# A conformer block on one core: the opening rebuilt on a transposed copy of x, three gate tiles moved to the front, and the fifth score row cut at another column

## The chip, the cores and the metric

The kernel runs on one core of a Trainium2 chip. TensorE (PE in the profile; PEld is its weight load) multiplies, VectorE (DVE), ScalarE (ACT) and GpSimd (POOL) do the elementwise work, and SyncE (SP) issues most of the transfers. The metric is the device time of one execution in microseconds (us); lower is better.

## The reference

One block of a network on x, 1024 tokens by 1024 channels, all in float32. Cut to what matters here:

```python
h = rms_norm(x, norm1_g)              # x * rsqrt(mean(x*x)) * g, per token
z = h @ w_in                          # 1024 x 7168
glu_in, q, k, v, gate_logits = split(z)      # 2048, 1024, 1024, 1024, 2048 columns
a_val, a_gate = split(glu_in)
a = a_val * sigmoid(a_gate)
a = silu(rms_norm(causal_depthwise_conv(a, conv_w, conv_b), conv_norm_g))
y_a = a @ w_conv_out
o = dilated windowed attention of normalised q, k with v      # 16 heads
y_b = o @ w_attn_out
g_a, g_b = split(sigmoid(gate_logits + gate_b))
x = x + (g_a * y_a + g_b * y_b) @ w_out
h = rms_norm(x, norm2_g)
u_val, u_gate = split(causal_depthwise_conv(h @ w_up, ffn_conv_w, ffn_conv_b))
x = x + (silu(u_gate) * u_val) @ w_down
```

The norm factor rsqrt(mean(x*x)) is one number for each token, so it can be taken out of a product: `rms_norm(x, g) @ W` is the factor of the token times `(x * g) @ W`.

## The kernel before, in words

Every matrix is kept as a pair of reduced-precision floats (a high part, made by ACT with a copy, and a low part, made by DVE or POOL as the difference), and a product is three matmuls: high by high, high by low, low by high (HH, HL and LH in the code of the opening; `product` and `gemm_half` elsewhere). Activations lie transposed: channels in the 128 partitions, eight channel blocks k, two token halves of 512 columns. So one gate tile (128 output channels, all tokens) is 2 halves x 8 k x 3 = 48 matmuls of 512 columns.

The stages, in the order in which they run on PE:

- Opening, lines 295 to 548. Eight token tiles of x are loaded; `squares` (ACT, L335) sums the squares of each, `rstd_of` (DVE L104, POOL L105) makes the norm factor, `scaled` (DVE, L341) multiplies by the factor and by g (which two matmuls, L405, spread over the partitions), `turned` (PE, L349) transposes 128x128 blocks into PSUM, and `both` (ACT L359, DVE L362) makes the high and low parts hT. The first gated-unit tile, c=0, runs in between (`first_pair`, L372: a gate column block "g" and a value column block "v"), then c=1; `glu_end` (L487, L488) forms value times sigmoid(gate) and stores it to `dain[c]`. While PE does c=1, DVE and ACT make sums of the activation blocks (`whole`, `form_high`, `form_low`, L508, L518) that tiles 2 to 7 need: those are done in pairs with a seven-product scheme of the Strassen kind (`pair_weights`, `pair_first`, `pair_sums`, `pair_rest`).
- q, k and v (`gemm_tok`, L144), with the causal convolution of the gated unit's output beside it on DVE (`by_dve`, L625) and on ACT and POOL (`by_pool`, L617). The convolution reads `dain` back; its last sums of squares go into `sqacc` (L634), which PE reads in `pss` (L729); the factor is then spread over the partitions by eight matmuls with a scaled identity (`dg` and `psr`, L738, L739).
- Gate tiles (16 of them) and the convolution's output product (8 tiles, "co", `conv_out`): a generator, `side_steps`, hands them out in steps of three matmuls. 24, 8 and 20 steps (COVER) run before the attention.
- Attention, 16 heads of 8 score rows, in 128 slots whose order on ACT, DVE and PE is written out by hand. Row i has (i+1)*128 key columns; its product with q goes in pieces of at most 512 columns (`score`, L765, L766). A slot issues a row, then the softmax of a row, the transposes (`flip`, L785) and the products with v (`weigh`, L799, L800) of the row five slots before (BACK), and between them steps of `side_steps` at the rates in FILL (steps in slot n modulo 8). What is left of the generator runs after the last slot, while the attention's output is fetched, and the next product (`merge`, "yb") follows.
- Output product, second norm, the feed-forward part. The change does not touch these.

Inside a `manual_schedule` block each engine keeps the order of the code; elsewhere a planner orders the instructions of each engine by its own estimate of times. `issue_after` holds instructions behind a given one on its engine. A tile of a pool with `bufs=n` waits until one of n slots is free; PSUM pool `psB` has four slots of one bank.

Of the kernel before, what the change touches and what calls it, by code (L numbers as in the profile page):

```python
# [21 lines left out]
P = 128  # L22
# [12 lines left out]
FILL = (1.5, 3.4, 1.8, 1.9, 1.6, 3.0, 2.1, 2.2)  # L35
# [3 lines left out]
BY_POOL = (3, 6)  # L39

# [13 lines left out]
def block_kernel(ctx: ExitStack, tc: tile.TileContext, x, g1, g2, pack, mask,  # L54
# [140 lines left out]
    def side_steps(hT, da):  # L195
# [51 lines left out]
        for c in range(12):  # L247
            for half in range(2):
                gate(c, half)
# [12 lines left out]
        for i, (_, n, go) in enumerate(uses):  # L262
            while len(got) < min(len(keys), keys.index(n) + 3):
                k = len(got)
                if k >= 4 and last[keys[k - 4]] >= i:
                    break
                w = ask_weights(src[keys[k]], keys[k])
                got[keys[k]] = w, count[0]
            w, need = got[n]
            if n.startswith("co"):  # L270
                need = max(need, marks[(i - 32) // 4 % 2])
            while count[1] < need:
                one_piece()
            yield from go(w)
# [22 lines left out]
    with tc.tile_pool(name="ph0", bufs=1, reuse_waits="tile") as p0:  # L297
        tform = lambda n: pT.tile([P, 2, 4, 512], F32R, tag=n, name=f"h{n}")
        xn_all = pT.tile([P, 4, 1024], F32, tag="t1", name="xs")
        xn = [xn_all[:, tt % 4] for tt in range(8)]  # L300
        gb_all = pT.tile([P, 4, 1024], F32, tag="t2", name="gb1")
        gb1, g1r = gb_all[:, 0], gb_all[0:1, 1]
        r11 = pT.tile([P, 2, 4, 512], F32, tag="t4", name="r11")[:, 0]
        act.dma_start(g1r, g1.unsqueeze(0))
        xt = []
        for tt in range(8):
            if tt < 4:
                xx = wp.tile([P, 1024], F32, tag=("whi", "wlo")[tt // 2], bufs=4, name=f"x_{tt}")
            else:
                if tt % 2 == 0:  # L310
                    x2 = p0.tile([P, 2, 1024], F32, tag=("xa", "xb")[tt // 2 - 2], name=f"x_{tt}")
                xx = x2[:, tt % 2]
            sp.dma_start(xx, x[tt * P : (tt + 1) * P, :])
            xt.append(xx)
            if tt == 3:
                wfirst = [(c, n, stage(w_ch[c], n)) for c, n in ((8, "g0"), (0, "v0"), (9, "g1"), (1, "v1"))]
# [6 lines left out]
        upper = [hb1.tile([P, 2, 4, 512], F32R, tag=f"hb{a}1", name=n) for a, n in enumerate(("b12", "b22"))]  # L323
# [5 lines left out]
        glu = {(0, 0): halves(big_ps("glugv_00"))}  # L329
        third = big_ps("tp_2")  # L330
        st1 = p0.tile([P, 2, 8], F32, name="st1")
        tps = {}

        def squares(tt):
            act.activation(xn[tt], xt[tt], AF.Square, accum_out=st1[:, 0, tt : tt + 1])  # L335

        def spread1(tt):
            rstd_of(st1[:, 1, tt : tt + 1], st1[:, 0, tt : tt + 1], D, st1[:, 0, tt : tt + 1])

        def scaled(tt):  # L340
            dve.scalar_tensor_tensor(out=xn[tt], in0=xt[tt], scalar=st1[:, 1, tt : tt + 1], in1=gb1,  # L341
                                     op0=ALU.mult, op1=ALU.mult)

        def turned(tt):
            for kk in range(2):
                ps = third[:, kk * 512 : kk * 512 + 512] if tt == 2 else bank_ps(f"tp_{tt}_{kk}")
                for j in range(4):
                    k = kk * 4 + j
                    pe.transpose(ps[:, j * P : (j + 1) * P], xn[tt][:, k * P : (k + 1) * P], ident)  # L349
                tps[tt, kk] = ps.rearrange("p (a b) -> p a b", a=4)  # L350

        def part(tt, kk, a):
            half, c0 = tt // 4, (tt % 4) * P
            if half:
                return upper[kk][:, a, :, c0 : c0 + P]
            return h0[a][:, kk * 4 : kk * 4 + 4, c0 : c0 + P]

        def high(tt, kk):
            return act.activation(part(tt, kk, 0), tps[tt, kk], AF.Copy)  # L359

        def low(tt, kk):
            return dve.tensor_tensor(out=part(tt, kk, 1), in0=tps[tt, kk], in1=part(tt, kk, 0).bitcast(F32),  # L362
                                     op=ALU.subtract)

        def both(tt, kk):
            return high(tt, kk), low(tt, kk)

        def first_pair(half, ks, passes, which, c=0):
            o = glu[c, half][which]
            for wa, ha in passes:  # L370
                for k in ks:
                    pe.matmul(o, wfirst[2 * c + which][wa][:, k, :], hT(ha, half, k),  # L372
                              start=(k == 0 and (wa, ha) == (0, 0)), stop=(k == 7 and (wa, ha) == (1, 0)))

# [25 lines left out]
        ENG = mybir.EngineType  # L400
        HH, HL, LH = ((0, 0),), ((0, 1),), ((1, 0),)
        with tc.manual_schedule(engines={ENG.Activation, ENG.DVE, ENG.PE}):
            ps = [bank_ps(f"gb_{kk}") for kk in range(2)]
            for kk in range(2):
                pe.matmul(ps[kk], ones[0:1, :], g1r[:, kk * 512 : kk * 512 + 512], start=True, stop=True)  # L405
            for tt in range(4):
                squares(tt)
            dve.tensor_copy(gb1[:, 0:512], ps[0])
            spread1(0)
            dve.tensor_copy(gb1[:, 512:1024], ps[1])  # L410
            spread1(1)
            for tt in range(4):
                scaled(tt)
                turned(tt)
                if tt < 2:
                    spread1(tt + 2)
                if tt == 2:
                    both(0, 0)
            both(0, 1)
            both(1, 0)  # L420
            both(2, 0)
            wraw = [r for _, _, r in wfirst]
            names = [n for _, n, _ in wfirst]
            hl, wfirst = [], []

            def wtiles(n):
                hl.append([wp.tile([P, 1024], F32R, tag=t, bufs=4, name=f"{t}_{n}") for t in ("whi", "wlo")])
                wfirst.append([t.rearrange("p (a b) -> p a b", a=KT) for t in hl[-1]])

            for n in names[:2]:  # L430
                wtiles(n)

            def wlow(i):
                dve.tensor_tensor(out=hl[i][1], in0=wraw[i], in1=hl[i][0].bitcast(F32), op=ALU.subtract)

            act.activation(hl[0][0], wraw[0], AF.Copy)
            both(3, 0)
            act.activation(hl[1][0], wraw[1], AF.Copy)
            wlow(0)
            wlow(1)  # L440
            a, b = range(4), range(4, 8)
            first_pair(0, a, HH, 0)
            first_pair(0, a, HH, 1)
            first_pair(0, a, HL + LH, 0)
            first_pair(0, a, HL + LH, 1)
            squares(4)
            spread1(4)
            both(1, 1)
            both(2, 1)
            both(3, 1)  # L450
# [999 lines left out]
```

## Time and profile before

| | |
|---|---|
| median of 3 runs | 1747.34 us (1747.05 to 1747.51) |
| the profiled execution's own time | 1745.71 us |
| its span, first to last instruction | 1743.7 us |
| PE busy | 1731.3 us, 8176 matmul records |
| DVE, ACT, POOL busy | 1278.6, 867.2, 435.6 us |
| HBM read, written | 204.19 MB, 79.69 MB |

PE records are pipelined: a record of a 512-column matmul lasts 0.39 us while the next starts 0.23 us after it, so the distance from start to start is what a matmul costs. A float32 matmul that is not of the reduced kind leaves two records. An entry in square brackets at the end of a timeline row is idle time of that engine before the row, and what ended it.

### The profile page before, as it was taken

Reading aid. Unit: us, or ns where it says so; the run is one execution under the profiler, and the core shown is the slowest. Engines: PE = TensorE matmul, PEld = TensorE weight load, DVE = VectorE, ACT = ScalarE, POOL = GpSimd, SP = SyncE. Lnnn points to the kernel's source line nnn. Section 1 sums busy time; section 2 is a strip of 40 time slices with the busy share of each in tenths; the row PEclk is TensorE's granted clock in tenths of the full one; section 3 lists DMA queues with packets and bytes.
Section 4 is the critical chain, followed back from the end, with each engine's and each line's share of the span. In section 5 each row is a group of like instructions: output and inputs, shape, how many; then the busy total and the mean of one; then the engine's idle time right before and its main releaser. Section 6 shows DMA issues by size and latency. Waiting matters only on the chain.

```text
span 1743.7 us, 22762 instructions
## 1 busy us (share of the span) xinstructions
PE 1731.3 (99%) x8176; PEld 1440.1 (83%) x8176; DVE 1278.6 (73%) x1747; ACT 867.2 (50%) x1338; POOL 435.6 (25%) x318
## 2 busy tenths in 40 slices
PE   8999999999999999999999999999999999999999
PEld 6888888888888888888888888888888888878887
DVE  8999998996366666677654573787777776889863
ACT  6333555555266666567664342555445444543431
POOL 1376899999012222222210000000000000000000
PEclk9999999999999999999999999999999999999999
DMA  6223545345775556667356576632222222499851
GB/s 241 79 97 108 194 139 175 109 133 181 202 251 153 158 156 175 164 189 225 117 167 213 175 283 233 218 111 77 93 85 73 85 85 85 138 334 327 292 176 48
DMA packets 149410, 285.37 MB, mean 164 GB/s; under 512 B 12081, under 2 KB 61361, under 8 KB 149042
## 3 DMA queue, kind: packets, MB, share of 16 engines
q1 hardware_dynamic: 148144, 281.82, 49.7%
q10 hardware_dynamic: 1154, 2.10, 0.3%
q8 instruction: 64, 1.05, 0.3%
q14 instruction: 48, 0.39, 0.1%
HBM read 204.19 MB, written 79.69 MB: 163 GB/s over the span
## 4 chain that ended last, share of the span: by engine, by line
PE 98%; DMA 1%; ACT 0%; DVE 0%; POOL 0%; SPq 0%; issue 0%; DVEq 0%; ACTq 0%
PE qkv L144 15%; PE dx L1286 7%; PE xz L124 6%; PE xz L126 6%; PE xz L125 6%; PE dy L1286 5%; PE wo L144 5%; PE gate L116 4%; PE pp L785 4%; PE gate L118 3%; PE gate L117 3%; PE glugv L372 3%; PE y L126 2%; PE y L125 2%; PE y L124 2%; PE s L766 2%
## 5 line engine op out<-in xcount | busy, mean ns | idle before, releaser
L625 DVE SCALAR_TENSOR_TENSOR work<-apad,pk,work 128x1024 f32<-128x1024 f32 x174 | 223.7, 1286 | 3.2
L779 POOL TENSOR_SCALAR p<-p,st 128x128 f32<-128x128 f32 (+7 forms) x128 | 97.0, 758 | 315.0 <-DVE st L778 214.7
L81 DVE TENSOR_TENSOR pl<-pp,ph 128x512 fp32r<-128x512 f32 x192 | 100.8, 553 | 87.6 <-ACT ph L80 87.4
L80 ACT ACTIVATE ph<-pp 128x512 fp32r<-128x512 f32 x192 | 87.2, 489 | 120.9 <-PE pp L785 120.1
L617 POOL TENSOR_TENSOR part<-prod,part 128x1024 f32<-128x1024 f32 x58 | 140.6, 2424 | 5.1 <-ACT part L614 3.0
L770 DVE CUSTOM_DVE_ANT_0 p<-s,m 128x128 f32<-128x128 f32 (+7 forms) x128 | 96.4, 754 | 45.5 <-PE s L766 40.8
L144 PE MATMUL qkv<-hi_qkv,hT 128*128 128x512 f32 x384 | 115.9, 393 | 0.0
L1189 DVE SCALAR_TENSOR_TENSOR u<-u,pk 128x1023 f32<-128x1023 f32 x88 | 112.5, 1280 | 1.0 <-ACT u L1187 0.9
L775 ACT ACTIVATE p<-p,st 128x128 f32<-128x128 f32 (+7 forms) x128 | 99.4, 777 | 4.5 <-DVE st L770 3.6
L616 ACT ACTIVATE prod<-apad,pk 128x1024 f32<-128x1024 f32 x60 | 68.6, 1149 | 36.9 <-POOL part L617 36.9
L785 PE MATMUL pp<-ident,p 128*128 128x128 f32 x576 | 83.9, 272 | 0.0
L144 PEld LDWEIGHTS qkv<-hi_qkv,hT 128*128 128x128 f32 x384 | 71.5, 188 | 14.6
L81 DVE TENSOR_TENSOR lo_uv<-raw_uv,hi_uv 128x1024 fp32r<-128x1024 f32 x20 | 24.5, 1225 | 79.9 <-ACT hi_uv L80 79.9
L785 PEld LDWEIGHTS pp<-ident,p 128*128 128x128 f32 x576 | 70.1, 140 | 15.3
L144 PE MATMUL wo<-hi_wo,mT 128*128 128x512 f32 x256 | 80.1, 391 | 0.0
L799 PE MATMUL o<-ph,v 128*128 128x512 f32 x192 | 74.8, 393 | 1.5 <-DVE op L811 1.5
L124 PE MATMUL xz<-blk_t,hi_s3g 128*128 128x512 f32 x176 | 68.7, 390 | 0.7 <-ACT xc L1163 0.7
L144 PE MATMUL qkv<-lo_qkv,hT 128*128 128x512 f32 x192 | 69.3, 392 | 0.0
L124 PE MATMUL xz<-h2left,hi_uv 128*128 128x512 f32 x176 | 68.7, 390 | 0.0
L126 PE MATMUL xz<-h2left,lo_uv 128*128 128x512 f32 x176 | 68.5, 389 | 0.0
L125 PE MATMUL xz<-blk_t,hi_s3g 128*128 128x512 f32 x176 | 68.5, 389 | 0.0
L126 PE MATMUL xz<-blk_t,lo_s3g 128*128 128x512 f32 x176 | 68.5, 389 | 0.0
(397 smaller groups left out, 5094.1 us busy)
## 6 DMA issues: line engine op xcount, KB each, us to landing
wr<-w_down SPq DMA_DIRECT2D x45, 512.0 KB, 5.7
gr<-dff SPq DMA_DIRECT2D x62, 256.0 KB, 5.2
raw_qkv<-w_qkv SPq DMA_DIRECT2D x24, 512.0 KB, 3.7
dff<-u SPq DMA_DIRECT2D x22, 512.0 KB, 2.6
raw_uv<-w_up SPq DMA_DIRECT2D x21, 512.0 KB, 3.2
raw_ug<-w_up SPq DMA_DIRECT2D x20, 512.0 KB, 3.2
dv<-v SPq DMA_DIRECT2D x16, 512.0 KB, 3.2
raw_gt<-w_ch SPq DMA_DIRECT2D x16, 512.0 KB, 5.5
```

What stands on the lines that cost most here:

```text
L81: by.tensor_tensor(out=lo, in0=src, in1=hi.bitcast(F32), op=ALU.subtract)
L124: pe.matmul(o, wh[:, k, :], bh[:, k, :], start=(start and k == 0), stop=False, skip_group_check=not start)
L125: pe.matmul(o, wh[:, k, :], bl[:, k, :], start=False, stop=False, skip_group_check=not start)
L126: end = pe.matmul(o, wl[:, k, :], bh[:, k, :], start=False, stop=(k == 3), skip_group_check=not start)
L144: pe.matmul(ps, l, r[:, k % 2, :], start=(n == 1), stop=(n == 3 * KT))
L617: pool.tensor_tensor(out=a[:, CW - 1 :] if j == CW - 1 else part, in0=prods[j % 3], in1=part, op=ALU.add)
L625: dve.scalar_tensor_tensor(out=a[:, CW - 1 :] if j == CW - 1 else work, in0=a[:, j : j + T], scalar=w(c, j), in1=work, op0=ALU.mult, op1=A ...
L775: act.activation(pt, pt, AF.Exp, bias=st[:, 0:1], scale=-1.0, accum_out=st[:, 1:2])
L779: pool.tensor_scalar(pt, pt, st[:, 2:3], 1.0, op0=ALU.mult, op1=ALU.mult)
L785: pe.transpose(pp[:, qb * P : (qb + 1) * P], pts[qb][:, kt * P : (kt + 1) * P], ident)
L1189: dve.scalar_tensor_tensor(out=acc[:, d:], in0=src[:, : T - d], scalar=w(2 - d), in1=acc[:, d:], op0=ALU.mult, op1=ALU.add)
L1286: pe.matmul(banks[n], a[:, c], b[:, d], start=(start and i == 0 and m == 0), stop=(stop and i == nf - 1 and m == 2), skip_group_check=True)
```

## The change

- Host layout: a transposed copy `xT` of x (eight channel blocks of 128 x 1024) and `w_first` (the weights of gated-unit tiles 0 and 1, gate and value columns side by side) are passed in; g1 comes as a 128x8 column layout. x itself is still passed and still loaded in full, after xT.
- Tiles 0 and 1 multiply `x * g` (`hu`, high and low), without the norm factor. Tile 0 runs k by k as the blocks of xT land, both halves. 14 float32 matmuls of ones by ones (WARM) stand ahead of it on PE. The factor of all tokens is made once, from x, then spread over the partitions by eight transposes into `rows`; `glu_gate` and `glu_value` multiply PSUM by it.
- hT is made on DVE and ACT from xT, g and `rows`; no transposes of x are left on PE (64 before). The sums for tiles 2 to 7 are made in place from the unsplit blocks (eight large DVE operations instead of sixteen).
- Gate tiles 0 to 2 (EARLY = 3) run right behind the two gated-unit tiles, ahead of the pairs; `side_steps` begins with tile 3, and FILL is scaled by some 0.865.
- `score`: the fifth row (i = 4, 640 key columns) is cut into 384 + 256 columns instead of 512 + 128, at an offset of 128 columns in its PSUM tile.
- `psr`: eight transposes of a broadcast column instead of eight matmuls with a scaled identity.
- The program is built with `dynamic_dma_scratch_size=1024`.

```diff
-FILL = (1.5, 3.4, 1.8, 1.9, 1.6, 3.0, 2.1, 2.2)
+FILL = (1.30, 2.94, 1.56, 1.64, 1.38, 2.59, 1.82, 1.90)
+EARLY = 3
+WARM = 14
...
-        for c in range(12):
+        for c in range(EARLY, 12):
...
+        act.dma_start(g1c, g1)
+        for k0, k1 in ((0, 1), (1, 4), (4, 8)):
+            act.dma_start(raw1[k0 // 4][:, k0 % 4 : (k1 - 1) % 4 + 1], w_first[0, :, k0:k1])
+        for k in range(KT):
+            sp.dma_start(xk[k // 4][:, k % 4], xT[k])
+        for tt in range(8):
+            sp.dma_start(xt[tt // 4][:, tt % 4], x[tt * P : (tt + 1) * P, :])
+            if tt in (3, 5):
+                sp.dma_start(raw1[tt // 2 + 1], w_first[1, :, 2 * tt - 6 : 2 * tt - 2])
...
+            warm = bank_ps("warm")
+            for i in range(WARM):
+                pe.matmul(warm[:, 0:P], ones, ones, start=True, stop=True)
+            for k in range(KT):
+                i, ks = k // 4, slice(k % 4, k % 4 + 1)
+                first_high(0, i, ks)
+                act.activation(hu[0][i][:, k % 4], xk[i][:, k % 4], AF.Copy, scale=g1c[:, k : k + 1])
+                first_low(0, i, ks)
+                dve.scalar_tensor_tensor(out=hu[1][i][:, k % 4], in0=xk[i][:, k % 4], scalar=g1c[:, k : k + 1],
+                                         in1=hu[0][i][:, k % 4].bitcast(F32), op0=mul, op1=sub)
+                for passes in (HH, LH, HL):
+                    for half in range(2):
+                        first_steps(0, half, k, passes)
...
+            for tt in range(8):
+                if tt in (4, 6):
+                    first_high(1, tt // 2 - 2, every)
+                    first_low(1, tt // 2 - 2, every)
+                square(tt)
+            rstd_of(st1[:, 1], st1[:, 0], D, st1[:, 0])
+            early = [wpiece(w_ch[16 + c], f"gt{c}") for c in range(2)]
+            glu[1, 0] = [bank_ps(f"glugv_10{which}") for which in range(2)]
+            for k in range(KT):
+                first_steps(1, 0, k, HH + LH + HL, (0,))
+            for k in range(KT):
+                if k == 2:
+                    spread = [bank_ps(f"psr1_{half}") for half in range(2)]
+                    for tt in range(8):
+                        pe.transpose(spread[tt // 4][:, tt % 4 * P : tt % 4 * P + P],
+                                     st1[:, 1, tt : tt + 1].to_broadcast([P, P]), ident)
+                first_steps(1, 0, k, HH + LH + HL, (1,))
+            for half in range(2):
+                act.activation(rows[:, half * 512 : half * 512 + 512], spread[half], AF.Copy)
+            for half in range(2):
+                for i in range(2):
+                    for k in range(4):
+                        v = view(i, half)[:, k]
+                        dve.scalar_tensor_tensor(out=v, in0=v, scalar=g1c[:, 4 * i + k : 4 * i + k + 1],
+                                                 in1=rows[:, half * 512 : half * 512 + 512], op0=mul, op1=mul)
+                    b_high(i, half)
+                if half == 0:
+                    glu_gate(1, 0)
+                for i in range(2):
+                    b_low(i, half)
+                if half == 0:
+                    glu_value(1, 0)
+            glu[1, 1] = [bank_ps(f"glugv_11{which}") for which in range(2)]
+            for which in range(2):
+                for k in range(KT):
+                    first_steps(1, 1, k, HH + LH + HL, (which,))
+            for half in range(2):
+                glu_gate(0, half)
+            for half in range(2):
+                ends = glu_value(0, half)
+        spill(db12, upper[0])
...
+        with tc.issue_after(ends.ins):
+            early += [wpiece(w_ch[16 + c], f"gt{c}") for c in range(2, EARLY)]
+            for c in range(EARLY):
+                for half in range(2):
+                    early_gate(c, early[c], half)
+            glu_gate(1, 1)
+            glu_value(1, 1)
...
+            r11, r21, r12, r22 = (view(i, half) for half in range(2) for i in range(2))
+            tt_(r22, r22, r12, sub)
+            tt_(r12, r12, r11, sub)
+            tt_(r11, r22, r11, add)
+            form_high("t2", r11)
...
-            dg = p1.tile([P, P], F32, tag="dg", bufs=4, name=f"dg_{tt}")
-            dve.tensor_scalar(dg, ident, rs8[:, tt : tt + 1], None, op0=ALU.mult)
-            pe.matmul(psr[:, (tt % 4) * P : (tt % 4 + 1) * P], ones, dg, start=True, stop=True)
+            pe.transpose(psr[:, (tt % 4) * P : (tt % 4 + 1) * P], rs8[:, tt : tt + 1].to_broadcast([P, P]), ident)
...
-            s = big_ps(f"s_{h}_{i}")
-            for c0 in range(0, nk, 512):
-                n = min(512, nk - c0)
+            s = big_ps(f"s_{h}_{i}")[:, P if i == 4 else 0 :]
+            for c0, n in ((0, 384), (384, 256)) if i == 4 else [(c, min(512, nk - c)) for c in range(0, nk, 512)]:
...
-    nc = bacc.Bacc("TRN2", target_bir_lowering=False, num_devices=1)
+    nc = bacc.Bacc("TRN2", target_bir_lowering=False, num_devices=1, dynamic_dma_scratch_size=1024)
```

More of the change, by code (lines that the diff above doesn't have):

```diff
@@ L322, in block_kernel @@
         h0 = [hb1.tile([P, KT, 512], F32R, tag=f"hb{a}0", name=f"hT{a}0") for a in range(2)]
[L323 removed]
+        upper = [None, None]
         def hT(a, half, k):
@@ L358, in high @@
[L358 to L373, printed above, removed]
+        sub, add, mul = ALU.subtract, ALU.add, ALU.mult
```

279 lines of the change are left out of this document (98 added, 181 removed).

## The prediction

> **What bounds the kernel now.** I read the page's busy line and chain first, then busy times by stretch, then the opening instruction by instruction.
>
> ```profile
> PE 1731.3 (99%) x8176; PEld 1440.1 (83%) x8176; DVE 1278.6 (73%) x1747; ACT 867.2 (50%) x1338; POOL 435.6 (25%) x318
> PE 98%; DMA 1%; ACT 0%; DVE 0%; POOL 0%; SPq 0%; issue 0%; DVEq 0%; ACTq 0%
> 8.15:14.94 6.79, 5.72 (x33) 4.65 (x33) 6.01 (x9) 5.20 (x11) 2.06 (x2) 1.00 1.03 423
> 14.94:62.46 47.52, 47.52 (x224) 39.27 (x225) 46.61 (x47) 26.25 (x34) 2.20 (x4) 1.00 0.35 134
> 490.00:880.00 390.00, 390.00 (x2133) 332.30 (x2132) 257.68 (x645) 252.17 (x557) 94.54 (x126) 1.00 0.60 172
> 890.00:900.00 10.00, 8.53 (x44) 6.68 (x43) 6.76 (x12) 6.98 (x13) 0.00 (x0) 1.00 0.58 198
> ```
>
> The last four rows give, after the stretch and its length, busy time of PE, PEld, DVE, ACT and POOL, then granted clock, DMA share and GB/s. PE is the bound from 14.94 on: no idle time in the opening's second part nor in the attention (490 to 880), where DVE has 257.68 of 390 us. So only three things help: PE starting earlier, fewer PE instructions, or fewer waits. Work moved from one full stretch to another is worth nothing by itself.
>
> ```profile
> 3.20 0.33 PEld L405 LDWEIGHTS gb<-gb,ones 1*128 1x128 f32 x1 [0.52 <-issue]
> 4.05 0.33 PEld L405 LDWEIGHTS gb<-gb,ones 1*128 1x128 f32 x1 [0.52 <-issue]
> 8.15 1.57 PEld L349 LDWEIGHTS tp<-ident,xs 128*128 128x128 f32 x8 [3.76 <-DVE xs L341]
> 11.72 0.86 PEld L349 LDWEIGHTS tp<-ident,xs 128*128 128x128 f32 x8 [0.34 <-DVE xs L341]
> 14.94 1.20 PE L372 MATMUL glugv<-hT,whi_g 128*128 128x512 f32 x4 [0.16 <-ACT hT L359]
> 27.89 1.15 PE L349 MATMUL tp<-ident,xs 128*128 128x128 f32 x8
> 28.80 1.18 PE L372 MATMUL glugv<-hT,wlo_v 128*128 128x512 f32 x4
> 62.46 0.39 PE L124 MATMUL uxz<-hT,hi_v 128*128 128x512 f32 x1
> 1592.98 5.44 PE dy L1286 x24
> ```
>
> The reader is to see that the first matmul of real work begins at 14.94 and the pairs at 62.46, and that 24 dense matmuls cost 5.44 us, 0.227 each. The stretch between holds 192 of them, 43.5 us; the remaining 4.0 are the last 32 transposes, eight of which take 0.91 (27.89 to 28.80).
>
> **The change part by part.** The sum is made against the profiled execution, 1745.71 us, which is 1.6 below the median of 1747.34; I carry the difference over to the median.
>
> *Start of PE's real work.* Before, it waits for x, squares, factor, scaling and transposes. Now it needs one block of xT, one of w_first, and ACT.
>
> ```profile
> 0.72 0.52 ACTq L304 DMA_DIRECT2D gb<-g  x1
> 1.28 1.28 ACT L335 ACT_TABLE_LOAD   x1 [1.28 <-PEq L1442]
> DMA to landing us min/median/max: 3.3/8.3/10.7
> 608.63 0.39 ACT L80 ACTIVATE ph<-pp 128x256 fp32r<-128x256 f32 x1 [0.53 <-PE pp L785]
> L616 ACT ACTIVATE prod<-apad,pk 128x1024 f32<-128x1024 f32 x60 | 68.6, 1149 | 36.9 <-POOL part L617 36.9
> 476.86 1.37 PE L739 MATMUL psr<-dg,ones 128*128 128x128 f32 x10
> 477.99 0.47 PE L116 MATMUL gate<-hT,hi_gt 128*128 128x512 f32 x1
> ```
>
> ACT issues four transfers instead of one, at 0.52 each from 0.72: 2.8. The table load ends at 4.1, the weights' high part (256 columns, 0.39) at 4.5, x times g (1149 ns, a scale for each partition) at 5.65. The first xT block is issued at 0.72 like x before, whose fastest landing took 3.3 us: 4.0, in time; if w_first shares the wires evenly, some 4.7. PE meanwhile does the 14 warm-up matmuls, 28 records. Ten records took 1.13 us at full speed (476.86 to 477.99), 0.113 each; the third and fourth records of the g spread stand 0.85 apart for 512 columns, so 0.21 for 128. That makes 3.2 to 5.9 us from about 1.2: done between 4.4 and 7.1. I take a start at 6.3, between 5.7 (ACT) and 7.1 (warm-up all slow): -8.6 us.
>
> The two weight-load rows of the transposes, 1.57 and later 0.86 for the same eight, show PE at half pace after its idle time although the granted-clock column says 1.00 there. [...]
>
> *Tile 0 by blocks.* For each k, PE has 12 matmuls, 2.72 us; ACT some 1.5 (0.39 + 1.15); DVE 1.6 (0.34, half of a 512-column difference, and 1.28, a row below); the wires 0.66 MB, 1.6 us at 423 GB/s. All are hidden under PE.
>
> *Transposes.* 32 go from 14.94 to 62.46: -4.0 (the first 32 lie before 14.94 and are in the start). Eight spread transposes come: +0.9, and 0.1 for the switch.
>
> *The norm factor.* It needs all of x, behind xT, on SP's queue: 4.19 + 1.05 + 4.19 + 1.05 = 10.5 MB. At 423 GB/s from 2.0 the last tile lands at 27.
>
> ```profile
> L341 DVE SCALAR_TENSOR_TENSOR xs<-x,st,gb x8: 1277/1284/1293, 6.8 to 26.5; 128x1024 f32<-128x1024 f32 x8
> 471.53 1.65 POOL L105 TENSOR_TENSOR crs<-css,mhalf 128x8 f32<-128x8 f32 x1 [36.78 <-DVE css L104]
> 48.30 0.69 DVE L391 TENSOR_TENSOR s<-s,raw_v 128x512 f32<-128x512 f32 x1
> 48.91 0.69 DVE L391 TENSOR_TENSOR raw_g<-raw_v,raw_g 128x512 f32<-128x512 f32 x1
> 57.85 2.29 DVE L508 TENSOR_TENSOR plain_xa<-hT,hT 128x2048 f32<-128x2048 f32 x1
> ```
>
> The last square on DVE (1.28), a small operation and POOL's power (1.65) bring the factor at 30.3. PE has tile 0 until 28.1, 24 matmuls of tile 1 until 33.5, 6 more until 34.9, and only then the spread: 4.6 us of cover. If the wires gave less than 354 GB/s, PE would wait. [...]
>
> *Behind the spread.* It ends at 35.8. ACT copies the rows; DVE does eight scalings of 512 columns, 0.61 apart (48.30 to 48.91), until 41.5, the sigmoid's input until 42.1, two low parts of 2.2 each until 46.5, the value until 47.7, the second half's scalings until 52.6, its low parts at 54.8 and 57.0. PE runs out of tile 1's first half at 39.9. Its second half needs a PSUM slot: if the freed slot of the spread is taken, no wait; if it must be the one that the sigmoid's input frees, 2.2 us. No row shows which; neither excludes further short waits on DVE. I take 1.0, nearer to none because two slots are free by 37. The gate tiles then begin at 50.8 + 1.0; their second half needs parts ready at 54.8 and 57.0, and PE gets there at 57 and 60. The sums for the pairs are eight operations of 2.2 us, 18 us, under 32.6 us of gate matmuls.
>
> *Gate tiles moved.* 3 x 48 matmuls, 32.6 us, come in front, and 48 steps of three go from the generator: FILL adds up to 280 steps over 128 slots before and 242 after, so 38 steps (25.9 us) leave the slots and 10 (6.8 us) the rest after them. Net 0, provided the attention gets shorter by its 26 us.
>
> ```profile
> 435.87 2.55 DVE L634 TENSOR_TENSOR sqacc<-sqacc,prod 128x1024 f32<-128x1024 f32 x2 [3.02 <-ACT prod L633]
> 469.41 1.84 PE L729 MATMUL pss<-ones,sqacc 128*128 128x1 f32 x16
> 893.87 0.50 PE L799 MATMUL o<-ph,v 128*128 128x512 f32 x1 [1.47 <-DVE op L811]
> 913.56 1.06 ACT L80 ACTIVATE hi_ao<-raw_ao 128x1024 fp32r<-128x1024 f32 x1 [1.56 <-DMA raw_ao<-w_ao]
> 927.12 0.39 PE L116 MATMUL yb<-oT,hi_ao 128*128 128x512 f32 x1
> ```
>
> Two covers shrink. The pairs and q, k, v move some 22 us later, and with them the convolution, but pss moves too and had 31 us to spare (438.4 to 469.4). The next product's first weights are ready at about 916 (913.56 + 1.06 and a DVE difference) and used at 927.12: 11 us of cover, 4 when 6.8 go. Both stay hidden; the wait of 1.47 at 893.87 stays.
>
> *Fifth row.*
>
> ```profile
> 596.67 0.39 PE L765 MATMUL s<-kh,q 128*128 128x512 f32 x1
> 597.30 0.45 PE L116 MATMUL gate<-hT,hi_gt 128*128 128x512 f32 x1
> 597.59 0.39 PE L117 MATMUL gate<-hT,hi_gt 128*128 128x512 f32 x1
> 600.37 0.28 PE L765 MATMUL s<-kh,q 128*128 128x256 f32 x1
> 600.60 0.40 PE L116 MATMUL gate<-hT,hi_gt 128*128 128x512 f32 x1
> 604.01 0.33 PE L765 MATMUL s<-kh,q 128*128 128x384 f32 x1
> 604.36 0.40 PE L116 MATMUL gate<-hT,hi_gt 128*128 128x512 f32 x1
> ```
>
> The row with 512 + 128 columns takes 0.63 us, and the gate matmul behind it 0.29 instead of 0.23: the 128-column matmuls leave a weight load uncovered. Two of 384 take 0.35, two of 256 0.23: 0.58 against 0.69. 16 heads: -1.8.
>
> ```profile
> q1 hardware_dynamic: 148144, 281.82, 49.7%
> ```
>
> *psr.* 16 records, 0.113 each, 1.8, become eight transposes at 0.11: -0.9. The scratch size has no row; and the data (281.82 of 285 MB) go by a queue that the page calls hardware. I take 0, between -0.5 and +0.5.
>
> Sum: -8.6 - 4.0 + 1.0 + 1.0 - 1.8 - 0.9 = **-13.3**. Profiled execution 1732.4; median **1734.0**.
>
> **The rivals.**
>
> *The factor or what stands behind it on DVE comes late* (20%). For it: 10.5 MB must come ahead of it, DVE runs without a gap from 36 to some 80, and several waits there have 2 us of cover. Against: 423 GB/s measured, 4.6 us of cover for the factor. At 300 GB/s the last x tile lands at 37, the factor at 40.3, and PE waits 5.4: 1739.4. Several short waits give 1737 to 1744.
>
> *The attention does not give the time back* (7%), the one that ends slower. If ACT's and DVE's chain of a slot, not PE, sets the slot's length once filler is taken out, up to 25.9 us stay: 1760. It decides from half: 13.3 of 25.9 us kept makes no change. For it: ACT and DVE have 65% of the stretch, in a hand-written order where one late part stops PE. Against: PE has no idle time there, and with 28 us less DVE would be at 71%.
>
> *The start isn't as early* (5%): first block late behind w_first, warm-up long; PE begins at 10, 1737.7.
>
> **How the numbers follow.** The sum has 65% (3% I leave to causes that I can't name), its own range 1731 to 1736 (ends of start, slot and scratch). From 1730 to 1741 the sum, the early part of the first rival and the late start lie inside, about 82%. A measurement of this kernel tells some 0.2%, 3.5 us, from no change. Faster takes the sum, most of the first rival and the last: 0.85; same 0.07, from the first rival's end and a half-kept attention; slower 0.08.
>
> **What would show it.** First glugv matmul near 6.3; the pairs' first uxz near 83.5 to 84.5 (62.46 - 11.6 + 1.0 + 32.6 = 84.5 at most); no PE wait over 1 us between; 490 to 880 shorter by some 28 us with PE at 100%; fifth-row pieces of 0.17 and 0.115 each. Wrong would be: PE idle before the spread transposes (factor late), PE waits on L799 or L800 in the slots (attention bound by its chain), a wait at the first yb (cover gone), or pss waiting for the convolution.

## The result, and the profile after

| | before | after |
|---|---|---|
| median | 1747.19 us (1746.71 to 1747.51, 4 runs) | 1735.22 us (1734.54 to 1736.44, 4 runs) |
| ratio after to before | | 0.9932, 95% interval 0.9920 to 0.9944 |
| the profiled execution's own time, its span | 1745.71, 1743.7 | 1734.54, 1732.7 |

The change makes the kernel 12.0 us faster by the medians, 11.2 by the two profiled executions; 1734.0 was predicted, from 1730 to 1741. The sum of the prediction, -13.3, is 2.1 too large against the profiled pair. Its terms erred in both directions, so they are gone through one by one.

First the busy line and the shares of the chain on the page of the changed kernel.

```profile
PE 1722.0 (99%) x8136; PEld 1435.4 (83%) x8136; DVE 1282.4 (74%) x1749; ACT 870.7 (50%) x1331; POOL 429.2 (25%) x311
PE 90%; DMA 5%; DVE 3%; ACT 1%; issue 0%; SPq 0%; POOL 0%; ACTq 0%; DVEq 0%; POOLq 0%
```

PE has 40 records fewer and is still the bound. The chain now passes through DMA and DVE for 8%, where it was PE for 98%: the fetch of `b_again`, for one, ends at 222.6 and is in it, though PE waits only 0.4 us for it. What stops PE is in the view of the waits by engine (total, times, longest):

```profile
PE glugv L344 <- ACT hu L388: 2.5, 1, 2.5
...
PE qt L645 <- DVE qn L637: 0.8, 1, 0.8
...
PE qkv L146 <- DMA b_again<-db: 0.4, 1, 0.4
...
PE wo L146 <- ACT hi_wo L881: 0.2, 1, 0.2
```

Left out are 1.0 us ahead of the first warm-up matmul and three waits of 0.3 to 0.7 us that the kernel before has too.

The opening by instruction (start, duration, engine and line; in brackets the idle time of that engine before the row and what ended it):

```profile
0.98 4.97 PE L384 MATMUL warm<-ones 128*128 128x128 f32 x28 [0.98 <-POOL ones L318]
...
6.98 0.42 ACT L335 ACTIVATE whi<-raw 128x256 fp32r<-128x256 f32 x1 [3.06 <-DMA raw<-w_first]
7.30 1.13 ACT L388 ACTIVATE hu<-xk,g1c 128x1024 fp32r<-128x1024 f32 x1
8.49 1.20 PE L344 MATMUL glugv<-hu,whi 128*128 128x512 f32 x4 [2.54 <-ACT hu L388]
...
31.76 1.67 POOL L107 TENSOR_TENSOR st<-st,mhalf 128x8 f32<-128x8 f32 x1 [30.32 <-DVE qkg L522]
...
37.18 1.03 PE L418 MATMUL psr<-ident,st 128*128 128x128 f32 x8
...
53.03 0.39 PE L118 MATMUL gate<-hT,hi_gt 128*128 128x512 f32 x1
```

The warm-up ends at 5.95, inside its predicted bounds. PE then idles 2.54 us, because ACT waited 3.06 us for the first slice of `w_first`; the first real matmul starts at 8.49, not at 6.3. From there no row up to 53.03 has an idle entry on PE: the factor is ready at 31.76 + 1.67 = 33.43, and the spread transposes start at 37.18, 3.75 us later.

Busy time of PE, PEld, DVE, ACT and POOL in the opening and in the attention, then granted clock, DMA share and GB/s:

```profile
8.49:53.03 44.54, 44.54 (x200) 36.96 (x201) 36.66 (x48) 26.20 (x33) 1.67 (x1) 1.00 0.68 270
494.40:880.00 385.60, 385.46 (x2133) 330.08 (x2132) 262.29 (x655) 256.86 (x560) 96.58 (x128) 1.00 0.64 185
```

Both are full on PE; DVE and ACT have 68% and 67% of the attention, up from 66% and 65%.

The stage borders are the first starts of three groups (after the semicolon of a row stands the shape; before it the first and the last start). After:

```profile
L702 PE MATMUL pss<-ones,sqacc x16: 164/250/250, 494.4 to 496.0; 128*128 128x1 f32 x16
...
L118 PE MATMUL yb<-oT,hi_ao x128: 389/389/389, 915.1 to 1001.5; 128*128 128x512 f32 x128
...
L126 PE MATMUL xz<-h2left,hi_uv x176: 389/389/473, 1095.7 to 1500.5; 128*128 128x512 f32 x176
```

Before, the first pss and yb stood at 469.41 and 927.12, and xz here:

```profile
L124 PE MATMUL xz<-h2left,hi_uv x176: 389/389/473, 1107.2 to 1512.0; 128*128 128x512 f32 x176
```

From these borders comes the balance. The end of the 192 gated-unit matmuls moves by 53.03 - 62.46 = -9.43. The three gate tiles put 144 matmuls, 32.65 us, ahead of pss, which moves by +24.99; so 24.99 - 32.65 + 9.43 = +1.8 is lost on the way. From pss to yb the time falls from 457.7 to 420.7: -37.0, of which -32.65 is the moved work and -4.4 a gain. From yb to xz it grows from 180.1 to 180.6, and from xz to the end of the span from 636.5 to 637.0: +1.0. Together -11.0, which is the difference of the spans.

### The profile page after: what moved, and what is told of

Read it like the earlier page. It is cut to its first block, busy times and chain, and to the rows that moved or that the text cites. A ratio compares the mean times of both kernels' runs of the same rounds, so it can differ in the third digit from the quotient of the medians.

```text
span 1732.7 us, 22673 instructions
## 1 busy us (share of the span) xinstructions
PE 1722.0 (99%) x8136; PEld 1435.4 (83%) x8136; DVE 1282.4 (74%) x1749; ACT 870.7 (50%) x1331; POOL 429.2 (25%) x311
## 4 chain that ended last, share of the span: by engine, by line
PE 90%; DMA 5%; DVE 3%; ACT 1%; issue 0%; SPq 0%; POOL 0%; ACTq 0%; DVEq 0%; POOLq 0%
PE qkv L146 14%; PE dx L1256 7%; PE xz L126 6%; PE xz L128 6%; PE xz L127 6%; PE dy L1256 5%; PE wo L146 5%; PE pp L755 4%; PE gate L118 3%; PE gate L120 3%; PE gate L119 3%; PE glugv L344 3%; PE y L127 2%; PE y L128 2%; PE y L126 2%; PE o L770 2%
```

## Experiments

The letters A to D in an expectation hold for that run, if it does not say otherwise. The kernel before ran beside each group: its medians were 1746.53, 1746.61 and 1746.88 us.

### What holds the first slice back

The slice has 128 KB and stands behind g (4 KB, 32 bytes to a partition) on ACT's queue; SP's queue starts with a block of xT of 512 KB. Three kernels move pieces between the two queues, and two more, made after their results, test what came out.

**The slice alone at the head of SP's queue.**

```diff
-        for k0, k1 in ((0, 1), (1, 4), (4, 8)):
+        sp.dma_start(raw1[0][:, 0:1], w_first[0, :, 0:1])
+        for k0, k1 in ((1, 4), (4, 8)):
```

> The changed kernel with only the first weight slice (k=0, 128 KB) moved from ACT's queue to the head of SP's. Theory A (a transfer of ACT's queue waits for a whole transfer of SP's each turn, so that the slice issued at 1.16 landed only at 6.98): the slice lands near 3.5, the first block of xT near 4.4, the first glugv matmul stands near 6.0 instead of 8.49; the slices k=1 to 3 stay on ACT's queue, one turn earlier than before, so a wait of at most 1 us at the second block; the first gate matmul near 51 instead of 53.03, the time some 2 us below the changed kernel's 1734.5 to 1736.4. Rival B (rows of 1 KB are slow wherever they are issued): the slice still needs over 5 us, first matmul at 8 or later, no gain. Rival C (the warm-up matmuls hold PE): first matmul not before 7.

Measured: 1736.01 us in one run. The slice landed at 3.5, but xT's block 0 only at 6.9, and the first glugv matmul started at 8.16 after 2.08 of idle. The wait changed its owner and lost little of its length. So A is refuted, and B too, since the slice took 2.8 us. C's time came out without its cause: the warm-up had ended at 6.1.

**All weights of tile 0 on SP's queue, in the order of need.**

```diff
-        for k0, k1 in ((0, 1), (1, 4), (4, 8)):
-            act.dma_start(raw1[k0 // 4][:, k0 % 4 : (k1 - 1) % 4 + 1], w_first[0, :, k0:k1])
+        ahead = {0: (0, 1), 1: (1, 4), 3: (4, 8)}
         for k in range(KT):
+            if k in ahead:
+                k0, k1 = ahead[k]
+                sp.dma_start(raw1[k0 // 4][:, k0 % 4 : (k1 - 1) % 4 + 1], w_first[0, :, k0:k1])
             sp.dma_start(xk[k // 4][:, k % 4], xT[k])
```

> The changed kernel with all three transfers of tile 0's weights on SP's queue, each just ahead of the xT block that needs it; g1c alone stays on ACT's queue. Theory A (turns between the queues): first glugv matmul near 6.0, no wait at the second block, the first gate matmul near 50.6, the time 2 to 2.5 us below the changed kernel, near 1732.8. Rival B (short rows are slow): first matmul at 8 or later and the same time as the changed kernel.

Measured: 1733.06 us (1732.33 to 1734.08, 5 runs), ratio to before 0.9921, interval 0.9907 to 0.9935. Its timeline:

```profile
5.58 1.15 ACT L390 ACTIVATE hu<-xk,g1c 128x1024 fp32r<-128x1024 f32 x1 [1.99 <-DMA xk<-xT]
...
6.79 1.20 PE L346 MATMUL glugv<-hu,whi 128*128 128x512 f32 x4 [0.98 <-ACT hu L390]
```

The slice landed at 3.1, block 0 at 5.5, PE began 1.70 earlier than in the changed kernel, and the first yb came 2.4 earlier. This is the fastest version that was run. Its interval overlaps that of the changed kernel; the earlier start in the trace says why it should be ahead, the times alone do not separate the two. A had the first matmul at 6.0 and the first gate matmul at 50.6, where 6.8 and 51.4 were measured; B, with 8 or later, is out.

**g at the head of SP's queue, the weights alone on ACT's.**

```diff
-        act.dma_start(g1c, g1)
+        sp.dma_start(g1c, g1)
```

> The changed kernel with g1c (4 KB, 32 bytes for each partition) moved from the head of ACT's queue to the head of SP's; the weight slices stay on ACT's. Theory A (one turn for each transfer, some 1.2 us, the time of one xT block): slice 0 is now first on its queue and lands about 1.2 us earlier, near 5.8, first glugv matmul near 7.3. Rival B (short rows are slow, turns do not matter): slice 0 near 6.9 as before, first matmul near 8.5.

Measured: 1733.79 us in one run. The DMA issues of the first 1.6 us (queue, count, size, us from issue to landing; the slice and g were issued at 0.73 and 0.72, the other two at 1.17 and some 1.2):

```profile
xk<-xT SPq DMA_DIRECT2D x1, 512.0 KB, 5.8
raw<-w_first ACTq DMA_DIRECT2D x1, 384.0 KB, 6.0
raw<-w_first ACTq DMA_DIRECT2D x1, 128.0 KB, 2.5
g1c<-g SPq DMA_DIRECT2D x1, 4.0 KB, 2.2
```

The slice came 3.7 us earlier than in the changed kernel (3.2 against 6.96); 1.2 was expected by A and nothing by B, so both fail. The first matmul still started only at 8.25, because block 0 paid for it: it landed at 7.0, together with the 384 KB transfer that stood second on the other queue. In the first kernel of this group it was the same pair, at 6.9 and 7.1. In the changed kernel the partners are g and block 0, which take 3.6 and 3.4 us from 0.72:

```profile
xk<-xT SPq DMA_DIRECT2D x1, 512.0 KB, 3.4
g1c<-g ACTq DMA_DIRECT2D x1, 4.0 KB, 3.6
...
raw<-w_first ACTq DMA_DIRECT2D x1, 128.0 KB, 5.8
```

So 4 KB took as long as 512 KB. A third theory, C, follows: the two queues advance in step, row by row; a transfer of 128 rows lands with the 128 rows that stand at the same place of the other queue, however large either is.

The record of the transfers shows the step itself. From 2 to 8.5 us of the changed kernel SP's queue (q1) and ACT's (q10) moved (packets, MB, share of the 16 engines' time):

```profile
q1 hardware_dynamic: 430, 1.58, 62.9%
q10 hardware_dynamic: 411, 0.51, 25.0%
```

By the sizes in the trace a packet is a row here, but for some of 4 bytes: q1 sent 386 rows of 4096 bytes and 44 packets of 4; q10 sent 128 rows of 32 bytes (g), 128 of 1024 (the slice), 121 of 3072 and 34 packets of 4. Each queue sent nearly as many as the other, while SP's carried three times the bytes.

**The slice at the head of ACT's queue, block 0 at the head of SP's, everything else behind.**

```diff
+        act.dma_start(raw1[0][:, :1], w_first[0, :, :1])
+        act.dma_start(g1c, g1)
+        ahead = {1: (1, 4), 3: (4, 8)}
```

(g's issue of before and the loop over three slices go; `ahead` is used as above.)

> ACT's queue carries only slice 0 of w_first (128 KB) and behind it g (4 KB); SP's queue carries xT block 0 first, then the rest of the weights in order of need. Theory A (a transfer waits for the bytes that are queued before it, whichever queue they are in): the same 640 KB are needed first as with everything on SP, so xT block 0 lands at 5.3 to 5.6, PE's first glugv at 6.6 to 6.9, the time within 0.5 us of the version with everything on SP (1733.1). Theory B (block 0 pays for standing behind the slice in its own queue, and g's short rows held ACT's queue only for what stands behind them): slice and g land by 4.5, block 0 at 4.2 to 4.6, first glugv at 5.8 to 6.2 and the time 0.7 to 1.0 us lower (1732.2).

Measured: 1734.06 us (1733.05 to 1736.73, 5 runs), ratio 0.9930, interval 0.9916 to 0.9944; not below the version with all on SP's queue. The issues:

```profile
xk<-xT SPq DMA_DIRECT2D x1, 512.0 KB, 4.4
raw<-w_first SPq DMA_DIRECT2D x1, 384.0 KB, 5.3
raw<-w_first ACTq DMA_DIRECT2D x1, 128.0 KB, 4.5
g1c<-g ACTq DMA_DIRECT2D x1, 4.0 KB, 5.5
```

The slice and block 0, both issued at 0.72, landed within 0.1 of each other; g and the 384 KB, both issued near 1.17, within 0.2. B here said 4.2 to 4.6 for block 0 and g by 4.5; block 0 came at 5.1, and g at 6.7 was the last thing that ACT needed, so that the first glugv started at 7.93. A, by bytes, had block 0 nearly right but not g. C is not among the theories of this expectation, so its pairs were read afterwards; the next run was made to test it.

**Block 0 in two halves, ACT's queue untouched.** If C holds, cutting a transfer on SP's queue into more rows brings the slice on the other queue forward.

```diff
         for k in range(KT):
-            sp.dma_start(xk[k // 4][:, k % 4], xT[k])
+            for c in ((0, 512), (512, 1024)) if k == 0 else ((0, 1024),):
+                sp.dma_start(xk[k // 4][:, k % 4, c[0] : c[1]], xT[k, :, c[0] : c[1]])
```

> The changed kernel with the first block of xT fetched as two halves of 512 columns (256 KB each); ACT's queue is untouched (g, then slice 0). Theory C (SP's and ACT's queues advance row by row, in step, so that two transfers of 128 rows land together whatever their sizes): g lands with the first half at 3.3 to 3.6, slice 0 with the second half at 5.0 to 5.6 instead of 6.96, PE's first glugv at 6.6 to 7.2 instead of 8.49. Theory D (g's short rows hold ACT's queue for some 3.6 us by themselves): slice 0 stays at 6.8 to 7.1 and the first glugv at 8.3 to 8.6.

Measured: 1735.77 us in one run. The issues up to 1.6 us; the slice was issued at 1.17 and landed at 5.6:

```profile
xk<-xT SPq DMA_DIRECT2D x2, 256.0 KB, 3.7
raw<-w_first ACTq DMA_DIRECT2D x1, 128.0 KB, 4.4
g1c<-g ACTq DMA_DIRECT2D x1, 4.0 KB, 3.4
```

The first glugv matmul started at 7.13, inside C's range and outside D's. The first pair came later than C had it, g at 4.1 and the half block at 4.0. Still C is the theory whose pairs hold in the changed kernel and these five: partners landed within 0.5 us of each other in the first two places, and 0.4 to 0.9 apart in the third. It does not make this version fast: the weights of blocks 1 to 3 landed at 9.9, PE waits a second time (1.27 us), and the gate tiles begin at 53.2. Why the queues would keep step is not shown.

**The warm-up.** Two kernels change only its length: WARM = 0 (and no PSUM tile for it), and WARM = 24.

```diff
-WARM = 14
+WARM = 0
```

> The changed kernel without the 14 warm-up matmuls. [...] Rival (the granted clock of 1.00 is the truth): the same pace from the first matmul, no change.

The rival stands against the slow start of the kernel before, where eight weight loads took 1.57 us after an idle time of PEld of 3.76 us, and eight from 11.72 on took 0.86.

Measured: 1736.87 us in one run, and in its timeline:

```profile
8.61 2.08 PE L344 MATMUL glugv<-hu,whi 128*128 128x512 f32 x4 [8.61 <-ACT hu L387]
...
11.94 1.99 PE L344 MATMUL glugv<-hu,whi 128*128 128x512 f32 x8
```

The first four matmuls take 2.08 us instead of 1.20. The first eight take 3.33 us from start to start, where the changed kernel takes 1.94 (8.49 to 10.43), and those from 11.94 run at full pace. The gate tiles begin at 54.5 instead of 53.0. Of these 1.5 us 0.1 is the later start; the warm-up is worth 1.4, and the rival is refuted. From the first matmul at 8.61 the slow stretch is 3.0 us long to the clock's first entry (11.61) and 3.3 to the matmuls at full pace (11.94).

In the kernel with g on SP's queue and in the one with the earlier FILL (below), the first four also took 2.08 and 2.07 us, after 2.12 and 2.25 of idle; in the changed kernel and the one with slice 0 on SP they took 1.20 after 2.54 and 2.08. So the length of the idle time alone does not say whether the half pace comes back.

The granted clock, asked for in short windows, shows more. In the kernel with g on SP's queue (window, its length, busy times as above, granted clock, DMA share, GB/s):

```profile
8.13:11.55 3.42, 3.30 (x8) 2.62 (x9) 2.66 (x3) 2.60 (x5) 0.00 (x0) 0.50 1.03 419
```

Here the first rise of the clock is at 4.72, the fall at 8.13, 3.41 us later, and PE was busy for 1.42 us between. In the changed kernel the entry of 1.00 lasts 1727.14 us from the rise at 4.31, in the kernel before 1733.97 us from 11.11: 506 and 508 times 3.413 us. In the kernel with the earlier FILL the clock fell 3.41 us after its rise as well, with 1.40 us busy between. It stayed at 1.00 in the changed kernel (1.63 us busy from 4.31 to 7.72) and in the one with slice 0 on SP (rise at 4.60, 1.49 us busy to 8.01). That is read from four executions and not tested, and it gives no limit: near the end of the attention of the kernel with the earlier FILL, at 922.9, the clock fell after 3.41 us in which PE was busy for 1.55. Ahead of the first rise the trace has no entry for the clock, and the view prints 1.00 there whatever the pace; without warm-up the first entry is at 11.61. This is why the prediction met half pace beside a clock of 1.00 in the kernel before, where the first entry is at 11.11.

The longer warm-up was to show whether the half pace is where the spread of the times comes from.

```diff
-WARM = 14
+WARM = 24
```

> The changed kernel with 24 instead of 14 warm-up matmuls, so that PE idles some 0.3 instead of 2.5 us before its first glugv. Theory A (after an idle time of 2.1 to 2.5 us PE sometimes starts at half pace, which costs 1.4 us: some runs of the changed kernel at 1734.5 and some at 1736.4): first four glugv in 1.20, first gate at 53.0, all times within 0.6 us of each other and the median 1734.5. Theory B (the pace after 2.5 us of idle has nothing to do with the spread of the times): the times spread over 1734.5 to 1736.5 as those of the changed kernel do; were the warm-up late, the first glugv would move to 8.6 to 8.9.

Measured: 1737.31 us (1736.41 to 1739.91, 4 runs), ratio 0.9948, interval 0.9931 to 0.9964. PE has no wait before the first glugv, which starts at 8.60 at full pace, and the gate tiles begin at 53.2. Yet the time is no better and spreads by 3.5 us, so A is refuted. The mean clocks of the changed kernel's timed runs don't sort their times either: 1736.44 and 1734.99 us with 0.999, 1734.54 and 1735.46 with 1.000. What is longer lies elsewhere, in its waits of PE:

```profile
PE wo L146 <- DVE lo_wo L882: 2.1, 2, 1.4
PE qkv L146 <- DMA b_again<-db: 1.1, 1, 1.1
```

Both hang on transfers. The weights of the output product come behind the merge's `gg` on ACT, which waited 5.59 us for its fetch in this execution where it waited 3.98 in the changed kernel. That the four timed runs are all above the changed kernel's median is not explained by the warm-up and stays open.

### What the gate tiles in front hide

**All of the change but the three tiles in front.**

```diff
-FILL = (1.30, 2.94, 1.56, 1.64, 1.38, 2.59, 1.82, 1.90)
-EARLY = 3
+FILL = (1.5, 3.4, 1.8, 1.9, 1.6, 3.0, 2.1, 2.2)
+EARLY = 0
```

> All of the change but the three gate tiles in front (EARLY = 0, and FILL as before). Theory A (the gate tiles are the cover under which VectorE makes hT's low parts and the sums for the pairs, which end at 61 and near 90 in the changed kernel): PE stops at 53 with the first products of the pairs and waits 13 to 18 us before the products on the sums; the time is 1745 to 1752, no better than before the change. Theory B (work moved from one full stretch to another is worth nothing): PE finds work all the same, the time is 1734 to 1737.

Measured: 1761.92 us in one run, above both ranges. Its waits of PE, and the window from the end of the gated-unit matmuls:

```profile
PE uxz L126 <- DVE sg L330: 9.1, 1, 9.1
PE uxz L128 <- DVE lo_v L83: 2.6, 1, 2.6
...
```

```profile
53.20:100.00 46.80, 28.28 (x90) 20.59 (x90) 39.89 (x36) 20.46 (x19) 13.23 (x9) 0.74 0.28 107
```

PE does 90 matmuls in 46.8 us, where 0.227 each would make 20.4; 26.4 us are lost. The waits in it add up to some 18; the rest is pace, with a granted clock of 0.74 in this window. So A is right and too low: the moved work is worth nothing by itself, but the new opening needs it as cover for DVE (40 of 47 us busy), and without it the whole change would be 15 us slower than the kernel before.

**The earlier FILL.** The generator, 48 steps shorter, runs at the rates of before.

```diff
-FILL = (1.30, 2.94, 1.56, 1.64, 1.38, 2.59, 1.82, 1.90)
+FILL = (1.5, 3.4, 1.8, 1.9, 1.6, 3.0, 2.1, 2.2)
```

> The changed kernel with FILL as before: the generator, shorter by 48 steps, runs empty in the slots, and nothing is left after the last slot. Theory A (the steps left over are the cover of the fetch of the attention's output and of the first weights of the next product, and the last slots lack filler): the first yb waits and the last slots stop PE; the time rises by 8 to 20 us to 1743 to 1755. Theory B (PE is busy in every slot whatever FILL says): no change, 1734 to 1736.

Measured: 1752.40 us in one run, as A said. The steps are used up at 911; the last transposes and products with v have no filler between them, and the first yb waits for its weights:

```profile
PE yb L118 <- ACT hi_ao L82: 7.4, 1, 7.4
```

```profile
912.00:928.40 16.40, 6.82 (x38) 4.71 (x36) 12.20 (x17) 12.84 (x21) 0.00 (x0) 0.83 0.41 139
```

In these 16.4 us PE is busy for 6.8, and the granted clock falls to 0.83. The steps left after the last slot are cover, as the prediction had it.

### How much the norm factor has to spare

Six copies of 512 KB, from x to a buffer in device memory that is not in use yet, stand ahead of x on SP's queue.

```diff
+        for tt in range(6):
+            sp.dma_start(dx2[tt], x[tt * P : (tt + 1) * P, :])
```

> The changed kernel with six copies of 512 KB (x to a buffer in device memory that is not in use yet, 3.1 MB) queued on SP behind xT and ahead of x: a test of the 3.75 us of cover that the norm factor has. Theory A (the factor comes when x has landed, and past 37.2 PE waits): at 0.42 MB/us for read bytes alone x lands 7.4 us later, the factor at 40.9 instead of 33.4, PE waits 3 to 9 us before the spread, also for tile 1's second weights, and the time is 1738 to 1744. Theory B (the queues have room, the copies run beside x): the factor stays before 37, the time 1734 to 1736.

Measured: 1740.57 us in one run, inside A's range. In the timeline:

```profile
34.02 0.80 PE L346 MATMUL glugv<-hu,whi 128*128 128x512 f32 x1 [3.16 <-ACT whi L337]
35.28 0.79 PE L346 MATMUL glugv<-hu,wlo 128*128 128x512 f32 x1 [0.46 <-DVE wlo L332]
...
40.85 1.67 POOL L107 TENSOR_TENSOR st<-st,mhalf 128x8 f32<-128x8 f32 x1 [39.41 <-DVE qkg L524]
...
44.60 1.03 PE L420 MATMUL psr<-ident,st 128*128 128x128 f32 x8
```

The factor comes at 42.5, 9.1 us later. But the spread has no wait: PE had stopped before, at the first matmul of tile 1, whose weights stand behind four tiles of x on the same queue and came late with them. After 3.16 us of idle, 14 matmuls went at about half pace until 40.9, at a granted clock of 0.51, which cost another 3.2; the gate tiles began at 60.5, 7.5 later than in the changed kernel (3.6 of waits, 3.2 of pace, 0.1 of the start, the rest not assigned). So the opening does hang on SP's queue, and its weakest place is tile 1's weights; had they been in time, the factor at 42.5 would have held the spread, which stood at 37.2.

### The fifth row alone

The kernel before, with only the other cut of the row:

```diff
-            s = big_ps(f"s_{h}_{i}")
-            for c0 in range(0, nk, 512):
-                n = min(512, nk - c0)
+            s = big_ps(f"s_{h}_{i}")[:, P if i == 4 else 0 :]
+            for c0, n in ((0, 384), (384, 256)) if i == 4 else [(c, min(512, nk - c)) for c in range(0, nk, 512)]:
```

> The kernel before with only the fifth row's cut at 384 + 256 columns. Theory A (a 128-column matmul costs more than its columns): the row takes 0.58 instead of 0.69 us, pss to the first yb is 455.9 instead of 457.7 (-1.8), with the wait of 1.47 near 893 still there, since it comes from DVE's and ACT's order in the slots of the merge, which this kernel does not touch. Theory B (the row's pieces are hidden behind other weight loads, and what shortened the attention in the changed kernel was the filler): 457.7, no change.

Measured: 1746.00 us in one run beside a median of 1746.88 (1744.98 to 1748.01), which decides nothing; the stages do. One row of it, with the gate matmul behind:

```profile
597.37 0.33 PE L764 MATMUL s<-kh,q 128*128 128x384 f32 x1
597.54 0.34 PE L765 MATMUL s<-kl,q 128*128 128x384 f32 x1
597.73 0.28 PE L764 MATMUL s<-kh,q 128*128 128x256 f32 x1
597.84 0.28 PE L765 MATMUL s<-kl,q 128*128 128x256 f32 x1
597.96 0.40 PE L116 MATMUL gate<-hT,hi_gt 128*128 128x512 f32 x1
```

The row takes 0.59 us, and the matmul behind it its usual 0.23. From pss (470.5) to the first yb (926.2) it is 455.7 us against 457.7: -2.0, of which some 0.4 is the wait on `op`, 1.0 here instead of 1.5. The 16 rows are thus worth 1.6 us; A holds.

## Why the prediction was right, point by point

The total lies inside the range and 1.2 us from the median, but partly because errors of both signs met.

- **Start of PE's real work: predicted -8.6, measured -6.45** (14.94 to 8.49). The term was mis-sized by 2.2, and the start lies outside the step's own bounds, 5.7 to 7.1. The step looked for the landing of xT's block and took the weight slice to be in time. The block came at 4.1, the assumed time; the slice came at 6.96: it stood second on ACT's queue, behind g (4 KB, 3.6 us), and from 2 to 8.5 us the two queues sent 430 and 411 packets, in step as theory C has it. The rival "the start isn't as early" named the w_first transfers, at 10; it was a smaller case of that, with the roles exchanged. That the sharing was near even in packets (430 and 411) and not in bytes (1.58 and 0.51 MB) is what the step lacked.
- **Warm-up**: 0.98 to 5.95, between the predicted 4.4 and 7.1.
- **Transposes and spread: predicted -4.0 + 1.0, measured -2.98** (47.52 to 44.54 for the same 192 matmuls).
- **Waits behind the spread: predicted +1.0, measured 0**. The PSUM slot was free.
- **Norm factor**: predicted at 30.3 with 4.6 us of cover, measured at 33.4 with 3.75. It came 3.1 later, and the spread 2.3 later with the late start; the transfers ran at 385 to 425 GB/s, as assumed, only from about 7 us on, not from 2 (175 between 5 and 6).
- **Gate tiles moved: predicted net 0.** The attention did give the time back: pss to yb is shorter by 37.0, its 48 steps are 32.65, and PE is full from 494.4 to 880. What was not foreseen is +1.8 ahead of pss: the waits on `qn` (0.8) and on `b_again` (0.4) are in the view of the waits and not in that of before; 0.6 is not assigned.
- **Fifth row and psr: predicted -2.7, measured -2.9**, what is left of -37.0 after the 48 steps and the next point. By the run of the row alone, 1.6 of it is the row (1.8 predicted); the rest, 1.3, would be psr (0.9 predicted), which no run has alone.
- **The wait of 1.47 at 893.87: predicted to stay, it went.** Before, DVE stood behind a merge operation that waited for its fetch, with `op` queued behind it:

```profile
889.32 0.69 DVE L893 TENSOR_TENSOR gg<-gg 128x512 f32<-128x512 f32 x1 [4.03 <-DMA gg<-dya]
...
893.14 0.68 DVE L811 TENSOR_TENSOR op<-o,ot 64x512 f32<-64x512 f32 x1
```

  After, the merge operation waits only 1.65 for ACT, and `op` runs ahead of the last products:

```profile
884.64 0.69 DVE L863 TENSOR_TENSOR gg<-gg 128x512 f32<-128x512 f32 x1 [1.65 <-ACT gg L861]
...
887.38 0.68 DVE L781 TENSOR_TENSOR op<-o,ot 64x512 f32<-64x512 f32 x1
```

  With the row cut alone the wait was still there (1.0), so the row is not what removed it. Nor is it the slower filler: the kernel with the earlier FILL has the old rates and no such wait, and with EARLY = 0 at the same rates the wait is there again (0.7). So it goes with the three tiles in front, by which the generator is 48 steps shorter; how that changes DVE's order there is not shown.
- **Cover of the next product's first weights: predicted 4 us, measured 1.6.** Their low part was ready at 913.5, the first yb at 915.1 had no wait.
- **Scratch size: predicted 0.** No run changes it alone, so this term stays open.
- **Behind the first yb: predicted 0, measured +1.0**, half between yb and xz (the wait on `hi_wo`, 0.2, and 0.35 more busy time for the same 817 matmuls, 180.14 against 179.79), half behind xz. In seven of the other kernels with the new opening PE waited between 0.3 and 2.3 us for the same weights, so this stretch differs from execution to execution by as much as the whole term.
- **First uxz at 83.5 to 84.5**: it stands at 69.4. The planner put first products of the pairs between the gate tiles; the mark was badly chosen, since the order there is the planner's. The mark that holds is the first gate matmul.
- **The rivals.** Late factor or DVE: did not happen, though the test with six copies shows that 9 us later it costs some 5, at another place than named. Attention not giving back: did not happen. With both the gate tiles and the rates undone the new opening ends on the other side (1761.92): that is a way to be slower which the prediction had not named, the lost cover of the pairs' sums.

## What to carry to other kernels

When two queues feed one start, lay out which transfers stand at the same place of both: in these runs a small transfer beside a large one landed with the large one (4 KB in 3.6 us, 512 KB in 3.4), and the one behind it later still (128 KB in 5.8). Put what is needed first into one queue in the order of need, with little on the other. Work that moves between full stretches changes nothing by itself, but ask what it hides in each place: here three gate tiles and the rates that go with them decided between 1735 and 1762.

## What the runs showed of the hardware

- 4 KB in 128 rows took 3.6 us beside a 512 KB transfer on the other queue, 3.4 us beside 256 KB, 2.2 to 3.0 us beside 128 KB (three runs), and 5.5 us in second place beside 384 KB. Two queues in use at once sent 430 and 411 packets, with 1.58 and 0.51 MB.
- After 2.1 to 2.5 us of idle, PE's first 512-column matmuls ran at half pace in two profiled executions (four in 2.07 and 2.08 us) and at full pace in two others (1.20); after 3.16 us, 14 of them stayed at about half pace, until 6.9 us after the first. The granted clock is 0.50 to 0.51 in windows over these slow matmuls; the slices of the page are 43 us long and don't show it. Ahead of the clock's first entry, 4.31 to 11.61 us after the start in the kernels above, the view reads 1.00 whatever the pace.
